# Low parts of the feed-forward gate weights: from VectorE to ScalarE and an adding DMA

## The chip, the cores and the metric

The kernel runs on one core of one Trainium2 chip. The metric is the device time of one execution in microseconds. TensorE (PE) multiplies, with its weight loads (PEld) beside it; VectorE (DVE), ScalarE (ACT) and GpSimd (POOL) do the element-wise work; SyncE (SP) issues the DMAs in the kernel before. Each engine takes its instructions strictly in its own order, and an instruction waits until what it reads has been written and what it overwrites has been read.

## The reference

Two layers, each of them a feed-forward block (FFN), a token-mixing block and a second FFN, for 512 tokens of 1024 channels in float32. The change touches the FFN alone:

```python
def _swiglu(x, w_in, w_out):
    gate, up = jnp.split(x @ w_in, 2, axis=-1)
    return (jax.nn.silu(gate) * up) @ w_out
# x: (512, 1024), w_in: (1024, 2 * 2816), w_out: (2816, 1024)
# per layer, with shift, scale and gate computed from a conditioning vector (adaLN):
h = h + 0.5 * ga1 * _swiglu(n1, w_in[l, 0], w_out[l, 0])
h = h + ga2 * _token_mixing(n2, ...)
h = h + 0.5 * ga3 * _swiglu(n3, w_in[l, 1], w_out[l, 1])
```

## The kernel before

**Products in three parts.** Every float32 factor is split into a high part (rounded to the type that TensorE multiplies, fp32r) and a low part, the value minus its high part. A product is then three matmuls: high by high, low of the activations by high of the weights, and high of the activations by low of the weights (`fm_steps`, in that order). For weights, `slab` (L219) does the split: it loads 128 rows by 1024 columns (512 KB) into a buffer `raw`, ScalarE writes `hi` (L185, a cast), and VectorE writes `lo` = `raw` - `hi` (L182).

**The FFN.** Its 2816 hidden channels are 22 tiles of 128, numbered f, in two halves of 11. For each f, `load` takes one gate slab and one up slab; TensorE runs 24 matmuls for the gate, then 24 for the up part; `act` takes silu on ScalarE (L419), the product with the up part on VectorE (L420), and splits the result into `hh` and `hl`. After each half, `residual` multiplies by `w_out`, whose slabs go into other tiles (`v`, `tm`), and updates `h`. Four FFNs run: FFN 1 and FFN 2 in layer 0 and FFN 3 and FFN 4 in layer 1, with the mixing block after FFN 1 and after FFN 3.

**The start of an FFN.** The gate and up slabs of f = 0 and f = 1 are loaded before the norm and multiplied side by side while the norm brings its channels (`norm_first`, by halves of the tokens; in FFN 1 in one piece). So all four of their `hi` and `lo` buffers are in use until the end of this stretch, and then f = 2 follows on TensorE at once.

**Buffers and order.** There are four buffers each of `raw`, `hi` and `lo` (L30), taken in turn by gate and up slabs. The buffers of the gate slab of f come free for that of f + 2. `raw` is shared with the adaLN vectors: `ada` (L247) loads a 512 KB tile of `ada_w` into a `raw` buffer and multiplies and sums it on VectorE (L259). Some FFN tiles do three of these each (`JN`), from f = 3 on in FFN 1, FFN 2 and FFN 3; the stretches where they run have the most DMA traffic. FFN 4 has none. TensorE's order is that of the code; the other engines' orders are set by a scheduler. SP issues all loads in one queue, so that a load that waits for its `raw` buffer holds those behind it.

GpSimd's work is small: in the norms it raises two columns to the power -1/2 (L300), and in the mixing block it normalises softmax rows.

Of the kernel before, what the change touches and what calls it, by code (L numbers as in the profile page):

```python
# [9 lines left out]
F32 = mybir.dt.float32  # L10
F32R = mybir.dt.float32r
# priorities and expected waits (us): they only set the order in which instructions are emitted
# [76 lines left out]
def f32(ap):  # L89
    return ap.bitcast(F32)  # L90
# [3 lines left out]
def trunk_kernel(  # L94
# [27 lines left out]
    # TensorE takes its instructions in the order in which they are emitted here  # L122
# [24 lines left out]
    # when a PSUM bank of a kind is likely to be free again  # L147
# [22 lines left out]
    # the time that TensorE needs for what has been emitted, for the order of what comes next  # L170
# [64 lines left out]

    def wk(slab_, k):
        return slab_[0][:, k * P : k * P + P], slab_[1][:, k * P : k * P + P]

# [10 lines left out]
    def ada(l, j, k, early=False):  # L249
        """One tile of 128 channels. Scale vectors become (1 + scale) * norm gain; the FFN gates  # L250
        take the factor 1/2, and the mixer's gate the 1/2 of sigmoid(x) = (tanh(x / 2) + 1) / 2."""
        m, b = mods[l][0][j], mods[l][1][:, j * 8 : j * 8 + 8]
        if early:
            raw = f32(vtile())
        else:
            raw = slabs.tile([P, SW], F32, tag="raw", name="raw", bufs=RAW)
        nc.sync.dma_start(raw[:, :D], ada_w[l, j, k])
        col = slice(k, k + 1)
        V.scalar_tensor_tensor(raw[:, :D], raw[:, :D], 1.0, cond, ALU.mult, ALU.mult, accum_out=m[:, col])  # L259
        if j % 3 == 0:  # L260
            V.tensor_tensor(m[:, col], m[:, col], b[:, col], ALU.add)
        elif j % 3 == 1:
            gi = (l * 3 + j // 3) * NK + k
            V.scalar_tensor_tensor(m[:, col], m[:, col], b[:, col], ng[:, gi : gi + 1], ALU.add, ALU.mult)
        else:
            V.tensor_scalar(m[:, col], m[:, col], b[:, col], 0.5, ALU.add, ALU.mult)
# [22 lines left out]
    def stat(acc, hf, sq=None):  # L289
        """1 / rms of 256 tokens, a column for each 128."""  # L290
        ps = bank(ps_o, "o")
        for t in range(2):
            c0 = (2 * hf + t) * P
            T.matmul(ps[:, t : t + 1], acc[:, c0 : c0 + P], C("ones"), start=True, stop=sq is None)
            if sq is not None:
                T.matmul(ps[:, t : t + 1], sq[:, c0 : c0 + P], C("ones"), start=False, stop=True)
        ms, rs = st(4, "ms"), st(4, "rs")
        with tc.high_priority(offset=AHEAD):
            V.tensor_scalar(ms[:, :2], ps[:, :2], 1.0 / D, EPS, ALU.mult, ALU.add)
            G.tensor_tensor(rs[:, :2], ms[:, :2], C("mhalf")[:, :2], ALU.pow)  # L300
        return rs

    def rows(rs):
        """The same on all partitions, tokens along the row."""
        pr = tt()
        for i, x in enumerate(rs):
            for t in range(2):
                c0 = (2 * i + t) * P
                T.transpose(pr[:, c0 : c0 + P], x[:, t : t + 1].to_broadcast([P, P]), ident)
        return pr[:, : 256 * len(rs)]  # L310
# [15 lines left out]
    def norm_first(l, j, nrm, run):  # L326
        """The norm by halves of the tokens, beside the first products that take it:
        run(half, hooks) emits them, and calls hooks[k] after channel tile k."""
        acc, pr = nrm
        n = norm_tiles()  # L330
        for k in range(NK):
            with tc.high_priority(offset=NPRI):
                norm(l, j, n, pr, HALVES[0], k)
        rs = []

        def second():
            pr = rows(rs)
            for k in range(NK):
                norm(l, j, n, pr, HALVES[1], k)

        run(n, 0, {1: lambda: rs.append(stat(acc, 1)), 4: second})
        run(n, 1, {})
        return n

    def fm_steps(ps, parts):
        """ps = sum of w^T x over (w hi, w lo, x hi, x lo)."""
        n = len(parts)
        for i, (wh, wl, xh, xl) in enumerate(parts):
            mul(ps, wh, xh, i == 0, False)
            mul(ps, wh, xl, False, False)  # L350
            mul(ps, wl, xh, False, i == n - 1)
            yield 0
# [17 lines left out]
    def residual(l, j, weights, xs, last, jobs, final=False):  # L370
        """h += gate * (x @ w); the last channels in two halves of the tokens, so that the norm
        of the first half runs beside the products of the second."""
# [24 lines left out]
    def ffn(l, s, nrm, jobs, first=False):  # L397
        j = 0 if s == 0 else 2
        n = None
        for half in range(2):  # L400
# [7 lines left out]
            def load(f):  # L408
                hid.append(hid_tiles(f))
                x = slab(w_in[l, s, f, 0]), slab(w_in[l, s, f, 1])  # L410
# [12 lines left out]
            if half == 0:  # L423
                # the first ones side by side, as the norm brings its channels
# [67 lines left out]
    def tm_chunk(nx, l, ci, ncols, evac):  # L492
        """Token-major projection: for each tile of 128 tokens, PSUM [tokens, ncols]."""
# [26 lines left out]
    def transposed(tm, h0, dup=False, hold=STACK):  # L520
        """[2 heads x 64, tokens] of heads h0, h0 + 1 (or of h0 twice)."""
# [15 lines left out]
    def q_stacks(ps, perm=False):  # L537
        """Per head of the pair, high parts and low parts of q on the two halves of the partitions."""
# [12 lines left out]
    def k_pair(ps, perm=False):  # L551
        """Per head of the pair, k on both halves of the partitions: high parts, low parts."""
# [27 lines left out]
    def halves(y, ps, e, vo=lambda x: x, vi=lambda x: x):  # L580
        """y[64 e:] = the sum of the two halves of PSUM's partitions."""
# [19 lines left out]
    def fill_bank():  # L601
        """PSUM for the fillers: once the chains are done, their banks as well."""
# [3 lines left out]
    def interleave(mains, fillers, width):  # L606
        """Emit chains of dependent steps, at most `width` of them at a time, and, where TensorE
        would wait for them, pieces of independent products. A chain yields the time until its
        next step can start, and the kind of PSUM bank that it takes. A (time, chain) of the
        lists may start when time() has come."""  # L610
# [47 lines left out]
    def mixing(l, nrm):  # L658
# [14 lines left out]
        def proj(src, out):  # L673
            """Feature-major projection to 128 columns."""
# [15 lines left out]
        def softmax_rows(units, mx):  # L690
            """exp of the tiles of scores, with their sums; maxima in mx."""
# [13 lines left out]
        # ======== native sparse attention  # L705
# [30 lines left out]
        # compressed keys and values: blocks of 32 tokens, 16 apart; column 31 is padding  # L736
# [9 lines left out]
        def blocks(pkv, j):  # L746
            """(high, low parts of 32 blocks) for each of the 16 pairs of tokens"""
# [89 lines left out]
        def ot_done(i):  # L837
            """[64, 4 heads, 128 queries] -> rows of two heads"""
# [54 lines left out]
        # selected branch (every block is selected: top_k = min(16, 8) of 8 blocks) and window  # L893
        # branch (the window of 512 spans the sequence): causal attention
# [46 lines left out]
        # ======== dilated attention: three groups of two heads  # L941
# [4 lines left out]
        def dil_proj(gi):  # L946
# [3 lines left out]
            if gi:  # L950
                # values: tokens by their residue mod 4
# [104 lines left out]
        # weights of the groups: softmax of their log-sum-exps  # L1056
# [51 lines left out]
        # ======== forgetting attention  # L1108
# [19 lines left out]
        def fox_gates():  # L1128
            """exp(-|f + bias|) for the six heads, and what log sigmoid and its running sum take after it"""
# [14 lines left out]
            def run():  # L1144
                """-8 x the running sum of log sigmoid"""
# [3 lines left out]
                # high parts on the first partitions, low parts from the 32nd on  # L1149
# [66 lines left out]
        # ======== merge gates, branch projections  # L1216
# [16 lines left out]
        def branch(q, d):  # L1233
            """acc[d] += (tanh gate + 1) * (y @ w)"""
# [76 lines left out]
    # the final norm: the first half of the tokens by channels, the second, which nothing hides,  # L1311
    # by tokens, with the gains taken in before its last channels are there
# [31 lines left out]
def _tiles(w, width):  # L1344
    """[K, N] -> [N / width, 128, K / 128 * width]: per slab of columns, the rows on partitions."""
# [4 lines left out]
def _layout(x, c, ada_w, ada_b, norm_g, final_norm_g, ffn_w_in, ffn_w_out, mix_w_in, nsa_cmp_pe,  # L1350
# [4 lines left out]
    # [L, 9 vectors, 8 tiles, 128 channels, 1024]  # L1355
# [35 lines left out]
    # [L, j, (token parity, dim), 16 pairs of tokens]  # L1391
# [14 lines left out]
def _result(got):  # L1406
    """The first half of the tokens comes by channels, the second by tokens."""
# [24 lines left out]
```

## Time and profile before

| | before |
|---|---|
| median of 2 runs | 2446.16 us (2444.4 to 2447.93) |
| span of the profiled execution | 2445.6 us |
| TensorE busy | 2363.8 us (97%) |
| VectorE busy | 1349.2 us (55%) |
| ScalarE busy | 930.3 us (38%) |
| GpSimd busy | 124.1 us (5%) |
| DMA, mean | 298.36 MB, 122 GB/s |
| mean granted TensorE clock | 0.993 |

The profile shows one execution. Its time lines give the start and length of each instruction, with the idle time of its engine ahead of it and what ended that in square brackets. Its waits say which engine stood still for which, and its windows give busy time, granted TensorE clock (1.00 is 2.4 GHz, 0.50 is 1.2 GHz) and the share of time in which the 16 DMA engines were busy. A matmul's length in the list is longer than its distance to the next, since matmuls overlap in the array.

### The profile page before, as it was taken

Reading aid. Unit: us, or ns where it says so; the run is one execution under the profiler, and the core shown is the slowest. Engines: PE = TensorE matmul, PEld = TensorE weight load, DVE = VectorE, ACT = ScalarE, POOL = GpSimd, SP = SyncE. Lnnn points to the kernel's source line nnn. Section 1 sums busy time; section 2 is a strip of 40 time slices with the busy share of each in tenths; the row PEclk is TensorE's granted clock in tenths of the full one; section 3 lists DMA queues with packets and bytes.
Section 4 is the critical chain, followed back from the end, with each engine's and each line's share of the span. In section 5 each row is a group of like instructions: output and inputs, shape, how many; then the busy total and the mean of one; then the engine's idle time right before and its main releaser. Section 6 shows DMA issues by size and latency. Waiting matters only on the chain.

```text
span 2445.6 us, 31894 instructions
## 1 busy us (share of the span) xinstructions
PE 2363.8 (97%) x12374; PEld 2016.5 (82%) x12374; DVE 1349.2 (55%) x2544; ACT 930.3 (38%) x1743; POOL 124.1 (5%) x192
## 2 busy tenths in 40 slices
PE   6999999999899999999999999999998999999998
PEld 4888889978678888888898888898877888888887
DVE  7756635576774567433367453356677645433333
ACT  3222324566563333223232223245566533322222
POOL 0000000021220000000000000001112100000000
PEclk9999999999999999999999999999999999999999
DMA  7856623311123337533247453332111232223222
GB/s 278 264 180 228 210 88 121 104 52 53 61 71 102 104 134 248 157 116 108 84 137 245 155 185 108 103 106 91 44 54 60 93 114 87 95 74 117 95 76 80
DMA packets 93055, 298.36 MB, mean 122 GB/s; under 512 B 11112, under 2 KB 20712, under 8 KB 92904
## 3 DMA queue, kind: packets, MB, share of 16 engines
q1 hardware_dynamic: 92904, 296.33, 36.8%
q8 instruction: 97, 1.59, 0.3%
q14 instruction: 54, 0.44, 0.1%
HBM read 289.99 MB, written 6.29 MB: 121 GB/s over the span
## 4 chain that ended last, share of the span: by engine, by line
PE 73%; DVE 11%; DMA 7%; ACT 5%; issue 3%; POOL 0%; SPq 0%; DVEq 0%; POOLq 0%; ACTq 0%
PE mm L174 62%; PE s L174 7%; DMA raw<-in_ada_w_dram 5%; DVE raw L259 2%; DVE lo L182 2%; PE o L174 2%; ACT p L695 1%; PE t L178 1%; DMA raw<-in_w_in_dram 1%; DMA raw<-in_w_out_dram 1%; ACT hi L185 1%; DVE ptl L182 1%; DVE k L182 1%; DVE p L569 1%; DVE v L259 0%
## 5 line engine op out<-in xcount | busy, mean ns | idle before, releaser
L174 PE MATMUL mm<-nh,hi 128*128 128x512 f32 (+1 forms) x1832 | 716.1, 391 | 25.6 <-DVE k L182 13.9
L174 PE MATMUL mm<-nl,hi 128*128 128x512 f32 (+1 forms) x1832 | 706.2, 385 | 2.9 <-DVE nl L324 2.9
L174 PE MATMUL mm<-nh,lo 128*128 128x512 f32 (+1 forms) x1832 | 705.6, 385 | 0.7 <-DVE lo L182 0.7
L185 ACT CAST hi<-raw 128x512 fp32r<-128x512 f32 (+3 forms) x402 | 320.7, 812 | 584.2 <-PE mm L174 301.3
L182 DVE TENSOR_TENSOR lo<-raw,hi 128x512 fp32r<-128x512 f32 (+3 forms) x402 | 376.0, 943 | 284.8 <-ACT hi L185 262.5
L174 PEld LDWEIGHTS mm<-nh,hi 128*128 128x128 f32 x1832 | 345.7, 189 | 98.7 <-issue 14.7
L174 PEld LDWEIGHTS mm<-nh,lo 128*128 128x128 f32 x1832 | 345.3, 188 | 70.6 <-DVE lo L182 2.0
L174 PEld LDWEIGHTS mm<-nl,hi 128*128 128x128 f32 x1832 | 345.6, 189 | 68.8 <-DVE nl L324 5.4
L174 PE MATMUL mm<-hh,v 128*128 128x512 f32 (+1 forms) x1280 | 342.8, 347 | 0.1
L174 PEld LDWEIGHTS mm<-hh,v 128*128 128x128 f32 x1280 | 226.4, 189 | 30.5 <-DVE h L389 0.3
L174 PE MATMUL mm<-hl,v 128*128 128x512 f32 (+1 forms) x640 | 221.8, 347 | 0.0
L259 DVE SCALAR_TENSOR_TENSOR raw<-raw,cond 128x1024 f32<-128x1024 f32 x128 | 156.1, 1223 | 114.6 <-DMA raw<-in_ada_w_dram 114.1
L182 DVE TENSOR_TENSOR v<-raw,v 128x1024 fp32r<-128x1024 f32 x80 | 98.0, 1224 | 156.7 <-ACT v L185 155.6
L185 ACT CAST v<-raw 128x1024 fp32r<-128x1024 f32 x80 | 84.2, 1053 | 243.7 <-PE mm L174 179.6
L420 DVE TENSOR_TENSOR v<-v,mm 128x512 f32<-128x512 f32 (+1 forms) x87 | 58.0, 667 | 208.8 <-PE mm L174 207.5
L174 PE MATMUL mm<-hh,tm 128*128 128x512 f32 (+1 forms) x480 | 136.2, 347 | 0.0
L174 PEld LDWEIGHTS mm<-hl,v 128*128 128x128 f32 x640 | 121.2, 189 | 15.2
L174 PE MATMUL mm<-hi,nh 128*128 128x256 f32 (+1 forms) x384 | 114.3, 298 | 5.6 <-DVE nb L573 3.4
L700 POOL TENSOR_SCALAR p<-p,den 128x128 f32<-128x128 f32 (+3 forms) x160 | 91.7, 591 | 434.8 <-ACT tm L669 98.5
L174 PE MATMUL mm<-hi,nl 128*128 128x256 f32 (+1 forms) x384 | 110.8, 289 | 0.0
L174 PE MATMUL mm<-lo,nh 128*128 128x256 f32 (+1 forms) x384 | 110.7, 288 | 0.0
L185 ACT CAST hh<-v 128x512 fp32r<-128x512 f32 (+1 forms) x94 | 55.3, 594 | 141.1 <-DVE v L420 141.1
(262 smaller groups left out, 3207.9 us busy)
## 6 DMA issues: line engine op xcount, KB each, us to landing
raw<-in_w_in_dram SPq DMA_DIRECT2D x176, 512.0 KB, 4.2
raw<-in_ada_w_dram SPq DMA_DIRECT2D x128, 512.0 KB, 4.3
raw<-in_w_out_dram SPq DMA_DIRECT2D x64, 512.0 KB, 3.7
raw<-in_w_mg_dram SPq DMA_DIRECT2D x48, 512.0 KB, 3.5
raw<-in_w_out_dram SPq DMA_DIRECT2D x64, 192.0 KB, 3.0
raw<-in_w_tm_dram SPq DMA_DIRECT2D x24, 512.0 KB, 3.5
raw<-in_w_fm_dram SPq DMA_DIRECT2D x18, 512.0 KB, 3.5
v<-in_ada_w_dram SPq DMA_DIRECT2D x16, 512.0 KB, 4.8
```

Of the source, the lines that this page charges most:

```text
L174: T.matmul(o, w, x, start=start, stop=stop)
L178: T.transpose(o, x, ident)
L182: V.tensor_tensor(o, a, b, ALU.subtract)
L185: A.copy(hi, src)
L259: V.scalar_tensor_tensor(raw[:, :D], raw[:, :D], 1.0, cond, ALU.mult, ALU.mult, accum_out=m[:, col])
L420: V.tensor_tensor(v, v, pu, ALU.mult)
L569: V.tensor_tensor_reduce(o, s, m, 1.0, -3.0e38 if first is None else first, ALU.add, ALU.max, acc)
L695: A.activation(x, x, AF.Exp, bias=nb[:, i : i + 1], scale=SCALE, accum_out=den[:, i : i + 1])
L700: G.tensor_scalar(x, x, r[:, i : i + 1], 1.0, ALU.mult, ALU.mult)
```

## The change

A second loader, `slab_by_dma`, takes the place of `slab` for the gate slabs that `load` fetches. ScalarE writes `hi` as before. Then ScalarE also writes `lo` = -`hi`, and GpSimd's queue issues a DMA that reads the same 512 KB of weights from memory a second time and adds them into `lo`. The result is the same value, weight minus high part. VectorE's subtraction falls away for these slabs. The up slabs, those of `w_out` and of the mixing block, and the first two gate slabs of FFN 1 (which are loaded elsewhere) stay with `slab`. So 4 x 22 - 2 = 86 gate slabs change. The rest of the diff removes comments.

```diff
+    def slab_by_dma(src):
+
+        raw = slabs.tile([P, SW], F32, tag="raw", name="raw", bufs=RAW)
+        nc.sync.dma_start(raw, src)
+        hi = slabs.tile([P, SW], F32R, tag="hi", name="hi", bufs=HI)
+        lo = slabs.tile([P, SW], F32R, tag="lo", name="lo", bufs=LO)
+        A.copy(hi, raw)
+        A.activation(lo, f32(hi), AF.Copy, scale=-1.0)
+        nc.gpsimd.dma_start(lo, src, accum_op=ALU.add)
+        return hi, lo
...
             def load(f):
                 hid.append(hid_tiles(f))
-                x = slab(w_in[l, s, f, 0]), slab(w_in[l, s, f, 1])
+                x = slab_by_dma(w_in[l, s, f, 0]), slab(w_in[l, s, f, 1])
                 if f > 2:
                     do(jobs, JN)
                 return x
```

ScalarE's order at the start of FFN 2, after the last piece of the norm (`nh`). In the kernel before, the casts `hi` are those of the slabs gate 2, up 2, gate 3, up 3, and `v` the silu of f = 0 and f = 1 (then of f = 2, 128x512):

```order
L323 ACTIVATE nh<-u,mod_6_99 128x256
L185 CAST hi<-raw 128x1024
L419 ACTIVATE v<-mm 128x256
L419 ACTIVATE v<-s 128x256
L185 CAST hi<-raw 128x1024 x2
L185 CAST hh<-v 128x256 x2
L185 CAST hi<-raw 128x1024
L419 ACTIVATE v<-mm 128x512
```

The same place in the changed kernel (L242 and L243 are the cast and the negated copy of a gate slab, L185 the cast of an up slab, L430 the silu; line numbers are 11 higher from `ada` on):

```order
L334 ACTIVATE nh<-u,mod_6_99 128x256
L242 CAST hi<-raw 128x1024
L430 ACTIVATE v<-mm 128x256
L430 ACTIVATE v<-s 128x256
L243 ACTIVATE lo<-hi 128x1024
L185 CAST hh<-v 128x256 x2
L185 CAST hi<-raw 128x1024
L242 CAST hi<-raw 128x1024
L185 CAST hi<-raw 128x1024
L243 ACTIVATE lo<-hi 128x1024
L242 CAST hi<-raw 128x1024
L430 ACTIVATE v<-mm 128x512
```

The negated copy of gate 2 stands behind the two silus, where the cast of up 2 stood; the casts of up 2, gate 3 and up 3 come later, and the cast of gate 4 now stands ahead of the silu of f = 2.

GpSimd's queue at the turn from the mixing block to FFN 2 in the changed kernel: the adding DMAs of the gate slabs 0 and 1, the two powers of the norm, then the DMAs of gate 2, 3 and so on (before, only the two powers stood here):

```order
L244 DMA lo_7755<-in_w_in_dram 128x1024
L244 DMA lo_7770<-in_w_in_dram 128x1024
L311 TENSOR_TENSOR rs_7705<-ms_7704,cst_86 128x2
L311 TENSOR_TENSOR rs_7860<-ms_7859,cst_86 128x2
L244 DMA lo_8095<-in_w_in_dram 128x1024
L244 DMA lo_8165<-in_w_in_dram 128x1024
```

The powers now stand behind the DMAs of the first two gate slabs.

TensorE's order at the same place, in the changed kernel: the last products of f = 0 and 1 (here those of up 1 with the last channel tile), then gate 2. It is unchanged, apart from the numbers in the names:

```order
L174 MATMUL s_7983<-nh_7794,hi_7776 128x256
L174 MATMUL s_7983<-nl_7795,hi_7776 128x256
L174 MATMUL s_7983<-nh_7794,lo_7777 128x256
L174 MATMUL mm_8105<-nh_7780,hi_8094 128x512
L174 MATMUL mm_8105<-nl_7781,hi_8094 128x512
L174 MATMUL mm_8105<-nh_7780,lo_8095 128x512
```

The third matmul of gate 2 reads `lo_8095`, the tile of the third DMA above.

## Rows read from the trace of the kernel before

**Rows 1.** The page: busy time, share of the span and instructions of TensorE
```profile
PE 2363.8 (97%) x12374; PEld 2016.5 (82%) x12374; DVE 1349.2 (55%) x2544; ACT 930.3 (38%) x1743; POOL 124.1 (5%) x192
```

**Rows 2.** Windows: busy us per engine, granted clock, DMA share, GB/s; FFN 1, FFN 2
```profile
200.00:300.00 100.00, 99.94 (x504) 85.31 (x503) 67.43 (x115) 27.80 (x35) 0.00 (x0) 1.00 0.71 237
1100.00:1200.00 100.00, 100.00 (x443) 82.81 (x442) 34.09 (x41) 27.76 (x37) 0.00 (x0) 1.00 0.27 87
```

**Rows 3.** Waits of TensorE inside FFN 1 and FFN 2: total us, times, longest
```profile
PE mm L174 <- ACT v L419: 1.2, 1, 1.2
...
PE mm L174 <- ACT v L419: 1.6, 3, 0.9
```

**Rows 4.** Time line of ScalarE in a quiet stretch of FFN 2
```profile
1103.31 1.05 ACT L185 CAST hi<-raw 128x1024 fp32r<-128x1024 f32 x1 [3.84 <-PE mm L174]
1104.26 0.59 ACT L419 ACTIVATE v<-mm 128x512 f32<-128x512 f32 x1
...
1114.18 1.05 ACT L185 CAST hi<-raw 128x1024 fp32r<-128x1024 f32 x1 [3.84 <-PE mm L174]
```

**Rows 5.** Time line where gate 2 of FFN 2 begins: ScalarE, VectorE
```profile
892.76 1.05 ACT L185 CAST hi<-raw 128x1024 fp32r<-128x1024 f32 x1 [7.84 <-PE mm L174]
894.25 2.00 ACT L185 CAST hi<-raw 128x1024 fp32r<-128x1024 f32 x2
...
893.84 1.23 DVE L182 TENSOR_TENSOR lo<-raw,hi 128x1024 fp32r<-128x1024 f32 x1 [8.40 <-PE s L174]
```

**Rows 6.** Time line of TensorE at the same place: gate 2's first low part
```profile
895.12 0.50 PE L174 MATMUL mm<-nh,lo 128*128 128x512 f32 x1 [0.24 <-DVE lo L182]
```

**Rows 7.** The same place in FFN 3 and FFN 4, and in FFN 1 (ScalarE, TensorE)
```profile
1260.92 0.50 PE L174 MATMUL mm<-nh,lo 128*128 128x512 f32 x1 [0.24 <-DVE lo L182]
...
2097.01 0.50 PE L174 MATMUL mm<-nh,lo 128*128 128x512 f32 x1 [0.24 <-DVE lo L182]
...
55.84 1.04 ACT L185 CAST hi<-raw 128x1024 fp32r<-128x1024 f32 x1
...
56.93 0.40 PE L174 MATMUL mm<-nh,lo 128*128 128x512 f32 x1
```

**Rows 8.** DMA issues: count, KB each, median us from issue to landing
```profile
raw<-in_w_mg_dram SPq DMA_DIRECT2D x48, 512.0 KB, 3.5
...
raw<-in_br_b_dram SPq DMA_DIRECT2D x2, 512.0 KB, 3.3
```

**Rows 9.** DMA from 200 to 300 us: the queue's packets, MB, share; issues
```profile
q1 hardware_dynamic: 6480, 23.60, 70.5%
...
raw<-in_ada_w_dram SPq DMA_DIRECT2D x25, 512.0 KB, 4.5
raw<-in_w_in_dram SPq DMA_DIRECT2D x20, 512.0 KB, 4.5
```

**Rows 10.** One issue on SP's queue; GpSimd's groups: busy us, mean ns
```profile
136.03 0.33 SPq L257 DMA_DIRECT2D raw<-in_ada_w_dram  x1
...
L300 POOL TENSOR_TENSOR rs<-ms,cst 128x2 f32<-128x2 f32 x14 | 12.1, 868 | 1777.6 <-DVE ms L299 1777.6
L1100 POOL TENSOR_TENSOR og<-og,ls 128x512 f32<-128x512 f32 x6 | 9.5, 1592 | 57.9 <-ACT ls L1091 57.9
```

**Rows 11.** TensorE's long wait in the mixing block; windows (granted clock third from last)
```profile
659.66 0.77 PE L174 MATMUL mm<-nh,hi 128*128 128x512 f32 x1 [6.93 <-DVE k L182]
...
654.00:655.00 1.00, 0.00 (x0) 0.00 (x0) 1.00 (x2) 0.32 (x1) 1.00 (x1) 0.99 0.00 0
655.00:656.00 1.00, 0.00 (x0) 0.00 (x0) 0.97 (x2) 0.25 (x1) 0.05 (x1) 0.50 0.00 0
...
665.00:666.00 1.00, 1.00 (x6) 0.77 (x5) 1.00 (x2) 0.47 (x1) 0.00 (x0) 0.89 0.00 0
```

**Rows 12.** ScalarE in FFN 2 where adaLN tiles are loaded too: casts of gate slabs
```profile
923.54 1.05 ACT L185 CAST hi<-raw 128x1024 fp32r<-128x1024 f32 x1 [1.79 <-DMA raw<-in_w_in_dram]
...
933.81 1.05 ACT L185 CAST hi<-raw 128x1024 fp32r<-128x1024 f32 x1 [1.33 <-DMA raw<-in_w_in_dram]
```

## The prediction

> **What bounds the kernel now.** Read the page's busy line first: TensorE works in 97% of the span, VectorE in 55%, ScalarE in 38%, GpSimd in 5% [rows 1]. Then read two windows inside the FFNs. In one with adaLN loads and in one without, TensorE is busy for 99.94 and 100.00 of 100 us at the full clock, while VectorE works for 67 and 34 us [rows 2]. In the quiet window 443 matmuls take 100 us, so that they follow each other every 0.226 us. Third, TensorE's waits inside the FFNs: after the norm of FFN 1 the largest is one of 1.2 us, and in the first half of FFN 2 three add up to 1.6 us, all for a silu that frees a PSUM bank [rows 3]. So VectorE's time is not what the FFN waits for, and hardly anything is there to be gained. What matters is whether the new `lo` still comes in time.
>
> **What is removed and added.** 86 subtractions of 1.23 us [rows 5] leave VectorE: 106 us that lie beside TensorE's work, worth nothing on the path. 86 negated copies go to ScalarE. The nearest row is the cast of the same shape, 1.05 us [rows 4], so 90 us are added to an engine that is busy 28 of 100 us there [rows 2]; a tile of 10.87 us has room for them. What is left is the adding DMA: GpSimd waits for the negated copy, issues, and TensorE waits for the landing. Call the time from the end of the negated copy to the landing X.
>
> **X.** No such DMA is in the trace, so it is bounded.
> - The issue: SP's takes 0.33 us; GpSimd's shortest group in the norm takes 0.87 us on two columns, its longest listed one 1.59 us [rows 10]. I take 0.87, since it is GpSimd that issues, with 0.33 and 1.59 as the ends.
> - The landing of 512 KB: 3.3 to 3.5 us in quiet stretches [rows 8], 4.5 us beside the adaLN loads [rows 9].
> - The second operand: the DMA also has to read `lo` itself. From 200 to 300 us the 45 loads of 512 KB kept the DMA engines busy for 70.5 us [rows 9], 1.57 us each. I add one such stream. The ends are nothing, and a whole second landing of 4.5 us.
>
> With adaLN loads, X = 0.87 + 4.5 + 1.57 = 6.9 us; without, 0.87 + 3.5 + 1.57 = 5.9 us. The low end is 0.33 + 3.3 = 3.6, the high end 1.59 + 4.5 + 4.5 = 10.6.
>
> Only a page prices a DMA from GpSimd's queue: the Trainium skill, DMA: Bandwidth & Descriptors, section "Anatomy of one DMA — SWDGE (gpsimd) path", fits 2.0 us plus bytes over 436 GB/s, which makes 3.2 us for a plain 512 KB; with X = 3.2 the sum below would end near 2470. No run here shows it.
>
> **Most gates are covered.** In a quiet stretch the cast of a gate slab starts when TensorE leaves that buffer, at 1103.31 us; the silu ends at 1104.85; the negated copy would end at 1105.9 [rows 4]. TensorE comes to that slab one tile and one up part later (10.87 + 5.44 us) and reads its low part in the third matmul, at about 1120.1 us. So 14.2 us of other products hide X, twice what it needs. If that cover were gone, each gate would cost X - 14.2.
>
> **Four gates are not.** At the start of each FFN, tiles 0 and 1 hold all four buffers until their last products, and gate 2 follows on TensorE at once. There the `lo` of gate 2 is on the path already: in FFN 2 the cast runs from 892.76, the subtraction starts at 893.84, and TensorE stands waiting for it until 895.12 [rows 5, 6]. FFN 3 and FFN 4 show the same wait of 0.24 us [rows 7]. In the changed order the negated copy takes the slot of up 2's cast, at 894.25, and ends at 895.30 [rows 5]. Then comes X, in which TensorE has nothing else: its order is fixed, and the next instruction is the one that waits. So each of these three FFNs loses X + 0.18 us. In FFN 1 the slot starts at 55.84 and ends at 56.88; TensorE reads that `lo` at 56.93 [rows 7]: it loses X. Sum: 3 x 6.9 + 5.9 + 0.5 = 27.1 us.
>
> **The clock.** A stop of this length has a second price. TensorE's wait of 6.93 us in the mixing block ends at 659.66, so it began at 652.73. The granted clock is 0.99 from 654 to 655 and 0.50 from 655 on, and the window from 665 to 666 has 0.89 [rows 11]: 1.2 GHz until about 665.2. From 659.66 that is 5.6 us of products at half speed, which loses 2.8 us. Even a stop as short as the low end of X, 3.6 us, is longer than the part of this one that lies before 655. Four times 2.8 makes 11.2 us. The mixing block's own waits are there before and after.
>
> **Edits at nothing.** At the turn to FFN 2 and FFN 4 (and FFN 2 to FFN 3) the powers of the norm stand behind the DMAs of gates 0 and 1 on GpSimd. Those DMAs wait for casts that run while the preceding output products still keep TensorE busy; without that cover the norm would be late by an issue, 0.9 to 1.6 us each. The cast of gate 4 now stands ahead of the silu of tile 2 and waits for its raw load; that load wins the time of the stop. Behind the stop nothing is late next: loads and casts get X more lead.
>
> **Sum.** 2445.6 us of span + 27.1 + 11.2 = 2483.9; the span is 0.6 us under the median of the runs, so 2484.
>
> **Rivals.**
> - *The DMA engines become the bound where adaLN loads run.* For it: five loads a tile keep them busy 70.5%, and two more streams make 7/5 of that, 98.7%. Where a gate's cast waits for its load, tiles follow at 933.81 - 923.54 = 10.3 us [rows 12], only 0.6 us under TensorE's 10.87. If both streams (3.1 us) came on top, less the 1.2 us by which `raw` is freed earlier without the subtraction, the pace would be 12.2 us: 1.3 us lost on each of 36 tiles with adaLN loads (17 in FFN 1, 8 and 11 in FFN 2 and FFN 3), 47 us, less the lead that three stops of 9.7 us give the loads, 29 us. So 2484 + 18 to 47: about 2515. Against it: one such DMA overlaps with some of the five loads only.
>  The Trainium skill speaks for this rival: Collectives: The Full Stack, section "The bandwidth ceiling: the fold count and why AG ≠ RS ≠ AR", says that an adding transfer is slower for its two source reads and not for the add, at about half the rate of a copy. By that rule the second stream is there in full, and so is the 98.7%; the trace has no adding transfer to agree or differ.
> - *The adding DMA is several times slower than a copy.* If X passed 14.2 us, nearly every gate would wait. At X = 18 some 74 gates lose 3.8 us each, and the four starts 84 us in all: about 2810. No row speaks for it but that none excludes it.
> - *Not slower.* The lighter VectorE and the earlier freed `raw` buffers take away the silu waits of [rows 3], 1.2 to 1.6 us for each half with adaLN loads, some 7 us in all: 2439. It decides only if gate 2's `lo` lands as early as the subtraction did, X under about 1 us, and even a plain load takes 3.3 [rows 8]; or if the scheduler had put other products there, which TensorE's unchanged order excludes.
>
> **How the numbers follow.** My forecast, four stops hidden nowhere else, has 0.60. With X at its low end (4 x 3.6 + 0.5 + 11.2 = 26, less up to 6 for the waits of [rows 3]) it reaches down to 2466; with X at 10.6 beside adaLN loads and 8.6 without (41 + 11) it reaches 2498, its own range. The DMA bound has 0.22, the slow DMA 0.08, not slower 0.05, something else 0.05. To hold 8 in 10, the range goes from 2466 to 2531, the upper end of the DMA rival. A measurement of this kernel tells 2% from no change, which is 2397 to 2495. Slower by over 2% are the DMA bound, the slow DMA and the upper tail of my forecast (0.06): 0.36. Faster by over 2%: 0.02. Within: 0.62.
>
> **What would show it.** In the changed profile: at four places TensorE waits 5 to 9 us for a DMA that writes `lo`, each followed by some 5.6 us at clock 0.50, and no other wait for `lo`; VectorE's busy time falls by about 106 us and ScalarE's rises by about 90; the DMA share in a window like 200 to 300 us rises from 0.71 to between 0.85 and 0.99 with TensorE still at 99%. I am wrong if those four waits are missing or shorter than 3 us, if the clock stays at 1.00 over them, or if waits for `lo` or for silu appear in other tiles.

## The result and the profile after

The changed kernel takes 2556.14 us, the median of 2 runs (2552.82 to 2559.47), beside 2446.16 us before: a ratio of 1.0453, with a 95% interval of 1.043 to 1.0475. The forecast was 2484 us, and its range ended at 2531. The profiled execution spans 2557.7 us at a mean granted clock of 0.976 (0.993 before).

The page of the changed kernel, its busy line, to be read against [rows 1]:

```profile
PE 2398.5 (94%) x12374; PEld 2036.2 (80%) x12374; DVE 1251.2 (49%) x2458; ACT 1012.4 (40%) x1829; POOL 199.9 (8%) x278
```

VectorE lost 98 us and ScalarE took on 82, as meant. TensorE issues the same 12374 matmuls but is busy 34.7 us longer, which is clock (0.976 for 0.993), and idle 159.2 us instead of 81.8. So 34.7 + 77.4 = 112.1 us of span have to be explained. The waits of TensorE, the two longest entries (who waited for whom: us in total, times, longest):

```profile
PE mm L174 <- DVE v L431: 55.8, 20, 5.5
PE mm L174 <- DMA lo<-in_w_in_dram: 25.2, 4, 6.5
```

The second line is the forecast: four waits for a `lo` that the adding DMA writes. The first is the surprise. L431 is the product `v * pu` in `act` (L420 before), whose end gives the PSUM bank of the up product back to TensorE. Before, TensorE never waited for it; now it does 20 times. They lie in the tiles that load adaLN tiles too; none lies in FFN 4, which has no adaLN loads. Together they make 81.0 us; less 2.9 us of silu waits that are gone (5.5 before, 2.6 now), that is the idle time to within a microsecond.

Windows of the changed kernel (span, busy us of the five engines, granted clock, DMA share, GB/s), with adaLN loads in the first two and without in the third, against [rows 2]:

```profile
100.00:200.00 100.00, 85.74 (x352) 68.83 (x351) 46.66 (x80) 25.32 (x33) 3.53 (x4) 0.95 0.64 194
200.00:300.00 100.00, 94.77 (x467) 80.07 (x465) 47.95 (x87) 28.08 (x33) 5.28 (x6) 0.97 0.75 230
1100.00:1200.00 100.00, 100.00 (x505) 85.53 (x504) 26.75 (x36) 34.34 (x41) 7.00 (x8) 1.00 0.61 164
```

In the quiet window TensorE loses nothing, although eight adding DMAs run there. Beside the adaLN loads it loses 5 to 14 us in 100, while the DMA engines' mean share is only 0.64 and 0.75. A mean over 100 us does not explain it.

VectorE's time line does. In the changed kernel, in FFN 1 (start, length, what it does, and in brackets the idle time ahead of it and what ended that):

```profile
107.25 1.23 DVE L270 SCALAR_TENSOR_TENSOR raw<-raw,cond 128x1024 f32<-128x1024 f32 x1 [0.85 <-DMA raw<-in_ada_w_dram]
...
110.14 1.22 DVE L270 SCALAR_TENSOR_TENSOR raw<-raw,cond 128x1024 f32<-128x1024 f32 x1 [1.46 <-DMA raw<-in_ada_w_dram]
...
117.12 1.23 DVE L270 SCALAR_TENSOR_TENSOR raw<-raw,cond 128x1024 f32<-128x1024 f32 x1 [5.55 <-DMA raw<-in_ada_w_dram]
...
118.47 0.69 DVE L431 TENSOR_TENSOR v<-v,mm 128x512 f32<-128x512 f32 x1
```

The product stands behind an adaLN multiply (L270) in VectorE's queue, and that multiply waits 5.55 us for its load. TensorE's line right after it:

```profile
119.20 0.50 PE L174 MATMUL mm<-nh,hi 128*128 128x512 f32 x1 [1.66 <-DVE v L431]
```

Why that load is late is shown by the chain of waits over the same stretch (start, length, what the chain runs through), before:

```profile
114.82 4.62 DMA raw<-in_ada_w_dram
119.46 1.25 DVE raw L259 x2
120.72 3.41 DMA raw<-in_ada_w_dram
124.16 1.25 DVE raw L259 x2
125.42 4.49 DMA raw<-in_ada_w_dram
```

and after:

```profile
103.89 3.34 DMA raw<-in_ada_w_dram
107.23 0.02 issue
107.25 1.25 DVE raw L270 x2
108.50 0.02 issue
108.52 8.58 DMA raw<-in_ada_w_dram
117.09 0.02 issue
117.12 1.24 DVE raw L270 x2
118.36 0.02 issue
118.38 3.44 DMA raw<-in_ada_w_dram
```

Each load starts when the multiply before it has freed one of the four `raw` buffers, so in each of these tiles two loads stand in series, one short and one longer. Before, a pair like 4.62 + 1.25 + 3.41 + 1.25 takes 10.5 us and just stays under TensorE's 10.87 us a tile. After, the longer one takes 8.58 us and the pair 14.5 us. It is longer because it does not run alone: GpSimd issues the adding DMA at 108.07, and the gate's and the up slab's loads are issued at 108.95 and 111.40. With two streams for the adding DMA that makes five of 512 KB; at 1.57 us each (from [rows 9]) an estimate of 7.9 us.

The mean share hides that the longer load lands in a burst. Windows of the changed kernel, in the last 6 us of that load and in the 4.7 us after it, then of the kernel before over its load of 4.62 us (the DMA share is second from last):

```profile
111.00:117.09 6.09, 6.09 (x28) 5.04 (x27) 0.53 (x3) 1.06 (x1) 0.00 (x0) 1.00 0.98 291
117.09:121.80 4.71, 3.05 (x14) 2.21 (x13) 3.74 (x6) 2.62 (x4) 0.00 (x0) 1.00 0.47 151
```

```profile
114.82:119.44 4.62, 4.62 (x22) 3.84 (x21) 2.56 (x4) 2.17 (x3) 0.00 (x0) 1.00 0.96 318
```

While several loads are in flight the DMA engines are nearly full, in both kernels; then their share falls, as the next loads wait for VectorE to free a buffer. The adding DMA makes the burst longer.

### The profile page after: what moved, and what is told of

Read it like the earlier page. It is cut to its first block, busy times and chain, and to the rows that moved or that the text cites. A ratio compares the mean times of both kernels' runs of the same rounds, so it can differ in the third digit from the quotient of the medians.

```text
span 2557.7 us, 32075 instructions
## 1 busy us (share of the span) xinstructions
PE 2398.5 (94%) x12374; PEld 2036.2 (80%) x12374; DVE 1251.2 (49%) x2458; ACT 1012.4 (40%) x1829; POOL 199.9 (8%) x278
## 3 DMA queue, kind: packets, MB, share of 16 engines
q0 software_dynamic: 12384, 45.09, 10.1%
## 4 chain that ended last, share of the span: by engine, by line
PE 66%; DMA 14%; DVE 11%; ACT 5%; issue 3%; POOL 0%; SPq 0%; DVEq 0%; POOLq 0%; ACTq 0%
PE mm L174 56%; DMA raw<-in_ada_w_dram 12%; PE s L174 7%; DVE raw L270 3%; PE o L174 2%; ACT p L706 2%; PE t L178 1%; DVE lo L182 1%; DMA raw<-in_w_out_dram 1%; DMA raw<-in_w_in_dram 1%; DVE ptl L182 1%; DVE p L580 1%; DVE k L182 1%; ACT hi L185 1%; DVE v L270 1%
## 5 line engine op out<-in xcount | busy, mean ns | idle before, releaser
L174 PE MATMUL mm<-nh,hi 128*128 128x512 f32 (+1 forms) x1832 | 731.0, 399 | 79.4 <-DVE v L431 55.8
L174 PE MATMUL mm<-nh,lo 128*128 128x512 f32 (+1 forms) x1832 | 718.0, 392 | 25.2 <-DMA lo<-in_w_in_dram 25.2
L174 PE MATMUL mm<-nl,hi 128*128 128x512 f32 (+1 forms) x1832 | 717.9, 392 | 2.2 <-DVE nl L335 2.2
L174 PEld LDWEIGHTS mm<-nh,hi 128*128 128x128 f32 x1832 | 353.6, 193 | 161.3 <-DVE v L431 64.5
L174 PEld LDWEIGHTS mm<-nh,lo 128*128 128x128 f32 x1832 | 352.7, 193 | 98.5 <-DMA lo<-in_w_in_dram 26.9
L174 PEld LDWEIGHTS mm<-nl,hi 128*128 128x128 f32 x1832 | 353.4, 193 | 70.8 <-DVE nl L335 4.9
L185 ACT CAST hi<-raw 128x512 fp32r<-128x512 f32 (+2 forms) x316 | 230.7, 748 | 271.9 <-PE mm L174 201.0
L182 DVE TENSOR_TENSOR lo<-raw,hi 128x512 fp32r<-128x512 f32 (+2 forms) x316 | 270.9, 867 | 123.0 <-ACT hi L185 119.5
L270 DVE SCALAR_TENSOR_TENSOR raw<-raw,cond 128x1024 f32<-128x1024 f32 x128 | 156.6, 1224 | 256.3 <-DMA raw<-in_ada_w_dram 256.1
L431 DVE TENSOR_TENSOR v<-v,mm 128x512 f32<-128x512 f32 (+1 forms) x87 | 58.0, 667 | 356.6 <-PE mm L174 327.7
L242 ACT CAST hi<-raw 128x1024 fp32r<-128x1024 f32 x86 | 90.6, 1053 | 261.6 <-PE mm L174 193.4
L244 POOL DMA_DIRECT2D lo<-in_w_in_dram x86 | 75.6, 879 | 1495.9 <-ACT lo L243 1425.8
L185 ACT CAST v<-raw 128x1024 fp32r<-128x1024 f32 x80 | 84.1, 1051 | 248.7 <-PE mm L174 180.3
L185 ACT CAST hh<-v 128x512 fp32r<-128x512 f32 (+1 forms) x94 | 55.4, 595 | 223.3 <-DVE v L431 223.3
```

Source lines behind the costliest of these rows:

```text
L174: T.matmul(o, w, x, start=start, stop=stop)
L182: V.tensor_tensor(o, a, b, ALU.subtract)
L185: A.copy(hi, src)
L242: A.copy(hi, raw)
L244: nc.gpsimd.dma_start(lo, src, accum_op=ALU.add)
L431: V.tensor_tensor(v, v, pu, ALU.mult)
```

## The experiments

The theory after this reading: the adding DMA makes one adaLN load per tile late, VectorE's queue passes that on to the product, and TensorE waits for a PSUM bank; the four stops come on top. Rivals: the new order of VectorE's and ScalarE's queues does it without any transfer; the DMA engines' throughput is the bound; the stops and the waits share one loss. The kernel before ran beside each set, with medians of 2447.77, 2448.55 and 2449.15 us.

**Only the quiet tiles.** The gates with adaLN loads still to come go back to VectorE:

```
-                x = slab_by_dma(w_in[l, s, f, 0]), ...
+                x = (slab_by_dma if f < 3 or not jobs else slab)(w_in[l, s, f, 0]), ...
```

> The adding DMA stays for gates 0 to 2 of each FFN and for the tiles after the last adaLN load of an FFN; the gates of the tiles with adaLN loads go back to the subtraction on VectorE. Theory (the adding DMA makes the adaLN loads land late, and their multiplies stand ahead of the product that frees the PSUM bank): the 20 waits for that product are gone, the four stops for lo of gate 2 stay, 2446 + 38 = 2484 us (2480 to 2490). Rival (the negated copy on ScalarE or GpSimd's queue costs in any tile): quiet tiles lose too, 2500 or more.

Measured 2477.37 us, ratio 1.012 [1.01, 1.0141]. No wait for the product is left; the four stops are there unchanged:

```profile
PE mm L174 <- DMA lo<-in_w_in_dram: 25.2, 4, 6.5
```

So the stops alone cost 30 us, 8 less than I had put on them, and the rest of the loss goes with the transfers beside the adaLN loads.

**The same without gate 2.** The condition is now `f < 2 or (f > 2 and not jobs)`.

> The adding DMA stays only where no adaLN load of the FFN is left to come, and for gates 0 and 1; gate 2 and the tiles with adaLN loads subtract on VectorE. Theory (the stops and the collision with the adaLN loads are all of the loss; a covered gate costs nothing): 2477 less the four stops of about 31 us, 2443 to 2450 us. Rival (the covered gates cost something too): 2455 us or more.

Measured 2447.95 us, ratio 0.9999 [0.9989, 1.0009]. 45 adding DMAs in covered places cost nothing. Between this run and the one above TensorE's idle time differs by 22.1 us: the four stops' 25.2 us less 2.6 us of silu waits (5.0 us here, 2.4 there) that the stops took away. Its busy time differs by 10.7 us (2366.5 and 2377.2). Of that, 8.1 us lie in the 40 products behind each stop, against the same products in the kernel before; the rest is clock elsewhere.

**Gate 2 alone goes back** (condition `f != 2`).

> Gate 2 of each FFN alone goes back to the subtraction. Theory (four stops and the waits for the product are two separate losses that add up): 2556 - 38 = 2518 us (2510 to 2525). Rival (the stops give the loads of the tiles that follow some lead, which is lost with them): the waits for the product grow, 2530 to 2547 us.

Measured 2533.17 us (2523.95 to 2541.03), ratio 1.0344 [1.0305, 1.0382]. That is 85 us more than the kernel before, and 23 us less than the changed kernel, not 38. The time lies in the rival's numbers, but the rival's mechanism is not seen: the waits for the product did not grow (43.6 us in 17, in the profiled execution, the fastest of the four). Nor can 23 us be told from the 30 of the stops alone, in runs that spread over 17 us. So the two losses add up within the spread, 85 + 30 = 115 for 110, and a lead that the stops give the loads is not shown; one of 29 us, which the prediction set against the DMA rival, does not fit these numbers.

**No DMA at all**, with the negated copy kept (the line with `accum_op` is left out).

> The adding DMA is left out, so lo keeps the negated high part and the output is not that of the reference; the negated copy on ScalarE stays. Theory (the DMA's transfer is what costs, both for gate 2 and beside the adaLN loads): 2440 to 2448 us, no wait for the product over 1 us. Rival (the new order of VectorE's and ScalarE's queues costs by itself): the waits for the product stay, 2556 - 38 = 2518 us.

Measured 2449.96 us, ratio 1.0011 [0.9995, 1.0026]. VectorE's queue is not quite that of the changed kernel, but the adaLN multiplies stand ahead of the product in it as well, and ScalarE has all its 86 copies. The waits for the product shrink to 4.9 us in five, the longest 2.1, where I had allowed 1 us. The new work of the engines costs nothing; the transfer does.

**A copying DMA in place of the adding one** (without `accum_op`; all queues in the same order).

> The DMA on GpSimd's queue copies instead of adding, at the same places and in the same order of all queues, so lo is the whole weight and the output is not that of the reference. Theory A (what costs is the second stream that the add reads): half the transfer, about half of the 72 us of waits for the product, and stops shorter by 1.6 us each: near 2515 us. Theory B (any sixth load of 512 KB beside the five does it, the add is free): 2545 to 2556 us. Theory C (a plain sixth load is hidden): 2475 to 2485 us.

Measured 2511.83 us, ratio 1.0274 [1.0213, 1.0334]. TensorE's waits:

```profile
PE mm L174 <- DVE v L431: 28.3, 15, 3.8
PE mm L174 <- DMA lo<-in_w_in_dram: 19.2, 4, 5.2
```

Half of the waits for the product are gone, with nothing but the add taken away. GpSimd's queue on the page (packets, MB, share of the 16 engines' span), first of the changed kernel, then of this one:

```profile
q0 software_dynamic: 12384, 45.09, 10.1%
```

```profile
q0 software_dynamic: 12384, 45.09, 5.8%
```

Over 86 transfers, 10.1% of 2557.7 us is 3.00 us of all engines for an adding DMA, and 5.8% of 2513.6 is 1.70 us for a copying one. The add costs 1.30 us of all engines, most of the second stream of 1.57 that I had added to X. By the Trainium skill, Collectives: The Full Stack, section "The bandwidth ceiling: the fold count and why AG ≠ RS ≠ AR", an adding transfer (there, of a collective) runs at about half the rate of a copy; by these two shares it is 0.57 of it, near that but not as slow.

**The transfer alone, in the kernel before.** VectorE keeps all its subtractions; beside each gate slab an adding DMA of 448 KB goes into a spare tile:

```
...
+    def extra(src, hi):
+        A.activation(spare_[:, :64], f32(hi[:, :64]), AF.Copy, scale=-1.0)
+        nc.gpsimd.dma_start(spare_, src[:, :896], accum_op=ALU.add)
...
                 x = slab(w_in[l, s, f, 0]), slab(w_in[l, s, f, 1])
+                extra(w_in[l, s, f, 0], x[0][0])
```

> The kernel before, with all its subtractions on VectorE, and beside each gate slab an adding DMA from GpSimd's queue of 448 KB into a spare tile that nobody reads (released by a copy of 64 columns on ScalarE behind the gate's cast). Theory A (the transfer alone makes the adaLN loads late, whatever the queue of VectorE looks like; no stops for gate 2): VectorE's product waits for an adaLN multiply here too, 2490 to 2520 us. Theory B (the old order of VectorE's queue stands the longer loads, only the new one does not): 2446 to 2460 us.

Measured 2518.62 us, ratio 1.0287 [1.0271, 1.0304]: 69 us for a transfer whose result nobody reads. It is no clean price, though. All these DMAs write the one spare tile, so the small copy that releases a DMA has to wait for the DMA before it, where gates follow each other closely at the start of an FFN. ScalarE's waits:

```profile
ACT spare L240 <- DMA spare<-in_w_in_dram: 45.1, 9, 6.8
```

TensorE's waits (the product is L428 here) and two pieces of the chain:

```profile
PE mm L174 <- DVE v L428: 46.1, 21, 5.6
...
97.04 8.66 DMA raw<-in_ada_w_dram
...
106.99 3.41 DMA raw<-in_ada_w_dram
```

The load of 8.66 us stands on a chain that began with two of the copy's waits, the last of which ended at 76.21. But the waits for the product go on in tiles in which no copy waits, for instance 1.16 us up to 133.15 and 2.03 us up to 158.40. So the transfer makes TensorE wait in the old order of VectorE's queue too; how much of the 69 us the experiment's own copies add was not taken apart.

**Where the late load meets the product.** The last of a tile's three adaLN multiplies is put behind the product in VectorE's queue (`prods` holds the products):

```
...
-                    do(jobs, JN)
+                    do(jobs, JN - 1)
+                    with tc.issue_after(prods[f - 2]):
+                        do(jobs)
```

> As the changed kernel, but VectorE's queue holds the last of a tile's three adaLN multiplies behind the product that frees the PSUM bank, no longer ahead of it. Theory (the ring sets the pace, and the product only shows it): the waits move to a later adaLN multiply or to the slabs' own loads, 2530 to 2560 us. Rival (only the place of that multiply in VectorE's queue): the waits for the product go, 2478 to 2495 us.

Measured 2496.17 us, ratio 1.0197 [1.0177, 1.0217]. My theory's numbers were wrong, the rival's nearly right. All bytes, the adding DMA and the four `raw` buffers are as in the changed kernel. The chain:

```profile
112.71 6.80 DMA raw<-in_ada_w_dram
119.53 1.25 DVE raw L270 x2
120.96 1.15 DVE raw L270 x2
122.28 0.68 DVE v L433
122.96 1.16 DVE raw L270 x2
124.13 7.43 DMA raw<-in_ada_w_dram
131.59 1.24 DVE raw L270 x2
```

The loads are nearly as slow as they were (6.4 to 7.8 us from 89 to 137 us; 6.2 to 8.9 for the longer ones of the changed kernel there), but only one stands in series per tile, and the three multiplies follow each other, with the product between them: 11.4 us from 112.71 to 124.13, against 14.5. The waits for the product are down to 3.3 us in three; silu is waited for 12.6 us in 15. So the ring of buffers does not set the pace by itself: what decides is how many loads VectorE's queue puts in series.

**Other buffers for the adaLN loads.** They land in the four buffers of `v`, idle in these tiles:

```
-                    do(jobs, JN)
+                    [ada(*jobs.pop(0), early=True) for _ in range(min(JN, len(jobs)))]
```

> As the changed kernel, but the adaLN loads of the gate tiles land in the four buffers of v, which are idle there, and not in the ring of raw; same bytes, same engines. Theory (the ring): gate and up loads no longer queue behind adaLN multiplies, the chain of two loads in series per tile is broken, and the four stops are left, 2478 to 2490 us. Rival A (the DMA engines' throughput is the bound, seven streams of 1.57 us a tile): no less than 2515 us. Rival B (an adaLN multiply on VectorE that waits for its late load ahead of the product is enough): waits for the product stay, 2530 to 2556 us.

Measured 2494.15 us, ratio 1.0184 [1.0162, 1.0206], just above what I expected. 5.3 us of waits for the product are left, in three. From 200 to 300 us the DMA share is 0.87 with TensorE busy 96.33, so over a tile the engines have room for its seven streams: their mean throughput was not the bound. The four stops grew to 35.9 us (one of 11.2), which is the 10 us above the theory's middle.

**Fewer adaLN loads a tile** (`JN = 2`).

> As the changed kernel, but two adaLN loads a tile instead of three (they are spread over more tiles; the number of loads is the same). Theory (the ring of four raw buffers: two loads in a row wait for one another in each tile, 3.4 us and 7.5 to 8.9 us, and the long one runs beside the adding DMA): four loads a tile leave the pace under TensorE's 10.87 us, the waits for the product shrink to under 15 us in all, 2484 to 2500 us. Rival (every tile with the adding DMA beside an adaLN load loses about 3 us, and there are now more such tiles): 2556 us or more.

Measured 2578.82 us, ratio 1.0531 [1.0498, 1.0564], slower than the changed kernel. My theory, that four loads in the ring would do, was wrong. The waits and the chain say why:

```profile
PE mm L174 <- DVE v L431: 64.2, 23, 5.3
...
106.83 6.62 DMA raw<-in_ada_w_dram
113.45 0.02 issue
113.48 1.25 DVE raw L270 x2
114.74 3.42 DMA raw<-in_ada_w_dram
```

With two multiplies a tile there are still two loads in series, 6.62 + 3.42, only in more tiles.

**Both remedies in the changed kernel** (adaLN loads into `v`, gate 2 on VectorE).

> The changed kernel with both remedies: the adaLN loads of the gate tiles land in the buffers of v, and gate 2 of each FFN subtracts on VectorE. Theory (late adaLN loads in the ring and the four stops are all of the loss): 2440 to 2452 us. Rival (other waits take their place, for instance lo of gate 3): 2460 us or more.

Measured 2460.61 us, ratio 1.0054 [1.0039, 1.007]. The theory was too good: 9.0 us of waits for the product (4) and 4.7 us for `lo` (3) take their place. 11 us above the kernel before are left of the 110.

**The kernel before, with the adaLN loads in the buffers of `v`.**

> The kernel before, with nothing changed but that the adaLN loads of the gate tiles land in the buffers of v. Theory (the silu waits inside the FFNs, 5.5 us in all, come from the ring of raw): 2438 to 2444 us. Rival (they come from elsewhere): 2446 to 2449 us.

Measured 2443.84 us, ratio 0.998 [0.9968, 0.9993]. TensorE's waits for silu, of which [rows 3] shows some, go from 5.5 us in eight to 2.5 in five. This beats both kernels, by 0.2%; the range of the theory was right at its upper end.

## Why the prediction was wrong

**Right: what bounds it, and the covered gates.** TensorE is the bound, the 106 us taken from VectorE bought nothing, and the covered gates cost nothing: 45 of them run in 2447.95 us.

**Right: the four stops.** TensorE in FFN 2, and the windows behind it:

```profile
946.77 0.79 PE L174 MATMUL mm<-nh,lo 128*128 128x512 f32 x1 [6.39 <-DMA lo<-in_w_in_dram]
...
951.00:952.00 1.00, 1.00 (x3) 0.77 (x3) 0.42 (x3) 0.00 (x0) 0.00 (x0) 0.50 1.10 274
952.00:953.00 1.00, 1.00 (x4) 0.77 (x3) 0.00 (x0) 0.00 (x0) 0.00 (x0) 0.70 1.01 262
953.00:954.00 1.00, 1.00 (x6) 0.81 (x5) 0.00 (x0) 0.00 (x0) 0.00 (x0) 1.00 1.02 266
```

The negated copy ends at 940.82, so X was 5.95 us there (forecast 6.9) and 5.94 in FFN 4 (forecast 5.9); in FFN 1 and FFN 3 it was 6.1. That the sum for a quiet stretch comes so near is partly luck. The DMA's issue starts 0.41 us after the copy's end (941.23), which the sum left out, and the data land 5.5 us after that start, with the issue of 0.94 us inside, where the sum put an issue in front of a landing that is counted from the start of its own issue.

The clock is at 0.50 for some 5.7 us behind the stops in FFN 2 and FFN 4, as [rows 11] had shown, but for only 3.1 and 3.5 us in FFN 1 and FFN 3. In FFN 1 the stop ends at 62.19:

```profile
65.00:66.00 1.00, 1.00 (x6) 0.83 (x5) 0.96 (x4) 0.00 (x0) 0.00 (x0) 0.93 0.97 303
```

The 40 products behind the four stops take 1.5, 2.7, 1.6 and 2.6 us longer than the same products in the kernel before, 8.4 us in all against 11.2. So of the 38 us, the stops' shorter waits (25.2 us for 27.1) take off 1.9, the clock 2.8 and the silu waits that the stops took away 2.6; 31 are left, beside the 30 that were measured alone.

**Wrong: "Behind the stop nothing is late next", and the price of the first rival.** The sum followed the adding DMA only to the one who waits for its own result. What it does to the five loads beside it was left to a rival at 0.22, and weighed by the mean share of the DMA engines: 98.7% full, 1.3 us on each of 36 tiles, less 29 us of lead. Three terms of that were off:
- The quantity. The mean share never came near 98.7% (0.64 to 0.75), and the loss came all the same. What counts is the landing time of the loads that stand in series, the longer one in a burst in which the engines are nearly full (0.98), and the median landing of the `w_in` loads rose from 4.2 to 5.9 us over the kernel.
- The size. To a pace of 10.3 us [rows 12] I added 3.1 and took off 1.2 for the subtraction that no longer holds `raw`. The measured pair of loads takes 14.5 us at 103.89, not 12.2, and without the stops of gate 2 the change costs 85 us, not 47.
- The lead. 29 us were set against it; the runs show none that stands out of their spread (85 + 30 us for 110).

"One such DMA overlaps with some of the five loads only" was the argument against that rival. It is true, and one is enough: the load that it overlaps with is the one that the product then stands behind. [rows 12] had shown the margin: 10.3 us of 10.87, in a chain of loads.

**Also missed: the clock of the shorter waits.** The wait of 3.22 us that ends at 104.72 is followed by 0.52; that of 1.66 us at 119.20 leaves it at 1.00:

```profile
106.00:109.00 3.00, 3.00 (x9) 2.34 (x8) 1.80 (x4) 1.72 (x3) 0.88 (x1) 0.52 0.71 224
...
119.00:120.00 1.00, 0.80 (x3) 0.67 (x4) 1.00 (x2) 0.81 (x2) 0.00 (x0) 1.00 0.70 156
120.00:121.00 1.00, 1.00 (x6) 0.82 (x5) 0.89 (x2) 1.00 (x2) 0.00 (x0) 1.00 0.88 344
```

Of the 34.7 us that TensorE is busy longer, some 8 belong to the stops; the other 26 lie in the FFN tiles in which it waits for the product.

**Of the marks named ahead**, three held: the four waits, VectorE's time (98 us less, for 106) and ScalarE's (82 more, for 90). The 5.6 us at clock 0.50 held behind two of the four stops. The DMA share from 200 to 300 us was to rise to 0.85 or more with TensorE at 99%; it is 0.75 at 94.77. Waits for `lo` or silu in other tiles were to show me wrong; the waits that came were for the product, which was not on that list.

## What to carry to other kernels

Price a new transfer twice: at its own consumer, and at every load that is in flight when it is issued, above all one that an in-order engine has to finish before it does something that the bottleneck waits for. The mean share of the DMA engines does not answer this; count the loads that stand in series per tile, with their landing times, and compare that sum with the bottleneck's time for a tile. If there is as little between the two as here (10.5 us against 10.87), a transfer "in the background" is on the path.

## What the runs showed of the hardware

- An adding DMA of 512 KB took 3.00 us of all 16 engines, a copying one 1.70; in a quiet stretch they landed in 5.5 and 4.5 us, while loads of the same size on SP's queue took 3.5 to 3.6.
- GpSimd spends 879 ns on issuing an adding DMA and 539 ns on a copying one of the same shape. By the Trainium skill, DMA: Bandwidth & Descriptors, section "Anatomy of one DMA — SWDGE (gpsimd) path", a plain 512 KB would take 3.2 us (an estimate from its fit); here it landed 4.5 us after the start of its issue, which itself took 0.54 us, in a quiet stretch with other loads about. The measurement decides: it is longer.
- Two lines of the changed kernel and of the run with the copying DMA show the issue (busy us, mean ns):

```profile
L244 POOL DMA_DIRECT2D lo<-in_w_in_dram x86 | 75.6, 879 | 1495.9 <-ACT lo L243 1425.8
```

```profile
L244 POOL DMA_DIRECT2D lo<-in_w_in_dram x86 | 46.4, 539 | 1475.6 <-ACT lo L243 1386.1
```
